# Another order of the query blocks in the attention stage of a two-layer trunk

## The chip, the cores and the metric

The kernel runs on one core of one Trainium2 chip. The metric is the device time of one execution in microseconds (us), as the median of several runs. The engines are TensorE (PE, with its weight loads as PEld), VectorE (DVE), ScalarE (ACT), GpSimd (POOL) and SyncE (SP), which issues the DMAs. Each takes its instructions in the order of the program.

## The reference

Two layers over x of shape (1, 1024, 1024) in fp32. Layer 0 is a gMLP and a pooling mixer, layer 1 a latent attention with 16 heads; each ends with an output projection, a residual and a layer norm. The change lies in the attention of layer 1, cut to this:

```python
    def attend_block(args):
        ql, qr, i = args
        s = jnp.einsum('bqhr,bkr->bhqk', ql, kv_c) + jnp.einsum('bqhd,bkd->bhqk', qr, k_rope)
        s = s.astype(jnp.float32) * ATTN_SCALE
        q_chunk = (i * Q_BLOCK + jnp.arange(Q_BLOCK)) // CHUNK
        mask = key_chunk[None, :] <= q_chunk[:, None]
        p = jax.nn.softmax(jnp.where(mask, s, -jnp.inf), axis=-1).astype(kv_c.dtype)
        return jnp.einsum('bhqk,bkr->bqhr', p, kv_c)

    o_lat = lax.map(attend_block, (q_lat_b, q_rope_b, jnp.arange(nb)))
    ...
    o = jnp.einsum('bshr,rhd->bshd', o_lat, w_uv).reshape(B, S, MLA_WIDTH)
    return (o * jax.nn.silu(z)) @ w_out
```

There are 8 blocks of 128 queries. Block i sees the keys of blocks 0 to i alone, so block 7 has eight times the scores of block 0. The blocks don't depend on each other, so they can be done in any order.

## The kernel before, in words

Precision: each fp32 operand of a product is kept as two parts, a rounded high part and the rest. `split` makes them from a PSUM tile (L120: a cast on ACT; L121: a subtraction on DVE), and `mm3` makes a product from three matmuls (L112 to L114).

The attention stage runs from about 910 us to 1377 us. The 16 heads are done in four groups of four; an item is one group g and one block i of queries, and there are 32 items in the order of the list `items` (L1745). An item has three generators, each of which is run in pieces:

- `gen_q`: for an odd block the latent queries of that block and the one below it (qlp, 24 matmuls, split into qlh and qll), then for every block the rotary part (qrp; rope on DVE and POOL; qrs; four transposes qrt; qrT).
- `gen_s`: for each of the four heads five score matmuls (L1785 to L1789; twice that for more than 512 keys) into a double PSUM bank sc. DVE masks the diagonal (L1821) and takes the maximum nm (L1824), ACT makes the exponential p with its row sum (L1832), DVE the reciprocal rz, POOL the normalised p (L1836). The blocks 1 and 0 do two heads in one tile sc, with lines of their own (L1798, L1800, L1804, L1809). There are two such double banks in all, so a tile sc takes the bank of the tile two before it, and that is free when the exponential has read it.
- `gen_v`: for each block j of keys four transposes of p (pt, L1853), split into pth, and three matmuls into av; the transposes run one block of keys ahead. Then av is split into oh and ol, and for an even block both blocks of the pair go through 12 matmuls uvp, are multiplied by the gate zt (L1877) and stored to o_d.

Tiles are named by group, block and head or key block: sc363 is group 3, block 6, head 3; pt110 is group 1, block 1, key block 0; oh31 is group 3, pair 1 (blocks 3 and 2).

A list of times places the pieces: item m's queries at about m, its scores at m + 2, its values at m + 3.3. So the scores of one item run beside the values of the item before it in the list. Group weights come once in a group, and the first loads and splits of the output projection (r1W, r1A; f1B00 and f1A00 are two of its operands) at fixed times near the end. From this the program's scheduler sets the order on every engine. After the attention comes the output projection, which reads o_d, then the residual and the layer norm.

Of the kernel before, what the change touches and what calls it, by code (L numbers as in the profile page):

```python
# [24 lines left out]
NG = H // GH  # L25
# [55 lines left out]
def trunk_kernel(ctx, tc, x, c, positions, ada_w, ada_b, ln_g, ln_b, e_w_in, gmlp_norm_g,  # L81
# [1621 lines left out]
    def gen_q(g, i, first, last):  # L1703
# [32 lines left out]
        for h in range(GH):  # L1736
# [4 lines left out]
        qrT[g, i] = qt  # L1741
        yield

    down = [7, 6, 5, 4, 3, 2, 1, 0]
    items = [(g, i, i % 2 == 1, i % 2 == 0) for g in range(NG)  # L1745
             for i in (down if g + 1 < NG else down[2:] + down[:2])]
    q_first = gen_q(*items[0])
    turns += [lambda: drain(q_first, 1) for _ in range(3)]

# [170 lines left out]
    for m in range(n):  # L1920
        g, i, first, last = items[m]
# [67 lines left out]
```

## Time and profile before

| | us |
|---|---|
| median of 3 runs (lowest to highest) | 1525.44 (1524.47 to 1526.9) |
| the profiled execution | 1528.2 |
| span of its trace | 1526.4 |
| PE busy in the span | 1478.0 (97%) |
| DVE, POOL, ACT busy | 1047.3, 652.0, 622.8 |
| mean granted clock of PE | 0.99 |

Busy time counts the instructions' own durations. Matmuls overlap, so two starts can be closer than the duration of one; what a matmul costs is the distance to the next start. The granted clock is a share of the full 2.4 GHz.

### The profile page before, as it was taken

The page shows a single profiled execution, that of the slowest core. Times are in us where ns is not written, and L with a number is a line of the kernel's source. Part 1 is how long each engine was busy: PE and PEld are TensorE (multiplying, and loading weights), DVE is VectorE, ACT ScalarE, POOL GpSimd, SP SyncE. Part 2 cuts the span into 40 slices and gives each one's busy share as a digit, 9 for nine tenths or more (in the row PEclk, how much of TensorE's full clock was granted, in tenths as well). Part 3 has the DMA queues.
Part 4 walks back from the last instruction along what each step waited for, and adds up shares of the span by engine and source line. Part 5 has one row for each costly group of instructions (what it writes and reads, how often), then busy time and mean ns, then how long its engine had stood idle before and what let it go on. Part 6 is the DMA issues. An engine that isn't in the chain of part 4 may idle for free.

```text
span 1526.4 us, 21181 instructions
## 1 busy us (share of the span) xinstructions
PE 1478.0 (97%) x7875; PEld 1269.7 (83%) x7875; DVE 1047.3 (69%) x1660; ACT 622.8 (41%) x1122; POOL 652.0 (43%) x583
## 2 busy tenths in 40 slices
PE   7999998999999999999999999999999999999997
PEld 5888776998898888888888878898989889878885
DVE  6557859574567596556766446777777777668598
ACT  3433323323323323425433445554544545555351
POOL 0033427376567023115776632454444442234245
PEclk9999999999999999999999999999999999999999
DMA  9725543103202799612375551131231131274532
GB/s 300 193 70 200 200 173 110 57 28 111 83 28 90 277 383 333 232 56 77 111 275 193 193 162 59 56 111 42 70 97 56 56 103 33 94 261 139 179 125 97
DMA packets 130771, 210.47 MB, mean 138 GB/s; under 512 B 11774, under 2 KB 78052, under 8 KB 130668
## 3 DMA queue, kind: packets, MB, share of 16 engines
q1 hardware_dynamic: 130668, 209.12, 40.5%
q8 instruction: 62, 1.02, 0.3%
q14 instruction: 41, 0.34, 0.1%
HBM read 152.46 MB, written 56.63 MB: 137 GB/s over the span
## 4 chain that ended last, share of the span: by engine, by line
PE 79%; DVE 9%; DMA 5%; issue 2%; ACT 2%; SPq 1%; POOL 1%; DVEq 0%; POOLq 0%; ACTq 0%
PE pt L1853 4%; PE y L113 3%; PE y L114 3%; PE y L112 3%; PE sc L1785 2%; PE av L113 2%; PE av L112 2%; PE av L114 2%; PE sc L1787 2%; PE sc L1786 2%; PE sc L1789 2%; PE sc L1788 2%; PE zb L113 2%; PE zb L114 2%; DVE mc L753 1%
## 5 line engine op out<-in xcount | busy, mean ns | idle before, releaser
L1836 POOL TENSOR_SCALAR p<-p,rz 128x1024 f32<-128x1024 f32 (+5 forms) x96 | 82.3, 858 | 175.3 <-DVE rz L1835 157.4
L120 ACT CAST pth<-pt 128x512 fp32r<-128x512 f32 x144 | 82.0, 590 | 79.9 <-PE pt L1853 78.9
L121 DVE TENSOR_TENSOR pth<-pt,pth 128x512 fp32r<-128x512 f32 x144 | 96.1, 687 | 24.6 <-ACT pth L120 23.7
L1832 ACT ACTIVATE p<-sc,nm 128x1024 f32<-128x1024 f32 (+5 forms) x96 | 81.8, 853 | 57.4 <-DVE nm L1824 45.9
L1824 DVE TENSOR_REDUCE nm<-sc 128x1 f32<-128x1024 f32 (+5 forms) x96 | 85.1, 887 | 2.0 <-DVE rz L1835 0.2
L1853 PE MATMUL pt<-ident,p 128*128 128x128 f32 x576 | 84.6, 272 | 0.1
L1853 PEld LDWEIGHTS pt<-ident,p 128*128 128x128 f32 x576 | 69.6, 140 | 11.3 <-DVE ol L121 0.3
L1785 PE MATMUL sc<-kvTh,qlh 128*128 128x512 f32 (+4 forms) x192 | 70.6, 368 | 8.3 <-ACT p L1804 3.2
L1431 POOL TENSOR_TENSOR ws<-ws,ws 128x1024 f32<-128x1024 f32 x16 | 43.4, 2724 | 75.0 <-DVE ws L1426 51.8
L1788 PE MATMUL sc<-KRh,qrT 128*128 128x512 f32 (+4 forms) x192 | 66.7, 348 | 0.0
L1789 PE MATMUL sc<-KRl,qrT 128*128 128x512 f32 (+4 forms) x192 | 66.4, 346 | 0.0
L1787 PE MATMUL sc<-kvTh,qll 128*128 128x512 f32 (+4 forms) x192 | 66.3, 345 | 0.0
L1786 PE MATMUL sc<-kvTl,qlh 128*128 128x512 f32 (+4 forms) x192 | 66.1, 344 | 0.0
L112 PE MATMUL av<-pth,kvh 128*128 128x512 f32 x144 | 61.1, 425 | 1.0 <-ACT pth L120 1.0
L113 PE MATMUL av<-pth,kvh 128*128 128x512 f32 x144 | 60.2, 418 | 0.2 <-DVE pth L121 0.2
L114 PE MATMUL av<-pth,kvl 128*128 128x512 f32 x144 | 56.7, 394 | 0.0
L753 DVE SCALAR_TENSOR_TENSOR mc<-mw,cT,mc 128x1024 f32<-128x1024 f32 x28 | 47.5, 1698 | 9.2 <-DMA mw<-in_ada_w_dram 8.8
L1245 POOL TENSOR_TENSOR r1A<-r1A,r1A 128x1024 f32<-128x1024 f32 x12 | 32.3, 2700 | 44.7 <-DMA r1A<-o_d 34.8
L121 DVE TENSOR_TENSOR ol<-av,oh 128x512 fp32r<-128x512 f32 x32 | 22.0, 687 | 39.7 <-ACT oh L120 39.7
L1785 PEld LDWEIGHTS sc<-kvTh,qlh 128*128 128x128 f32 x192 | 36.5, 190 | 14.6 <-ACT p L1832 5.6
L120 ACT CAST oh<-av 128x512 fp32r<-128x512 f32 x32 | 18.8, 587 | 60.1 <-PE av L114 59.7
L1550 POOL TENSOR_TENSOR qrf<-qrf 128x256 f32<-128x256 f32 x32 | 23.6, 737 | 44.6 <-DVE rz L1835 20.1
(1887 smaller groups left out, 5147.8 us busy)
## 6 DMA issues: line engine op xcount, KB each, us to landing
mw<-in_ada_w_dram SPq DMA_DIRECT2D x32, 512.0 KB
r0W<-in_e_w_out_dram SPq DMA_DIRECT2D x32, 512.0 KB
wf_d<-ws SPq DMA_DIRECT2D x28, 512.0 KB
r1W<-wf_d SPq DMA_DIRECT2D x28, 512.0 KB
ada<-in_ada_w_dram SPq DMA_DIRECT2D x32, 256.0 KB
r0A<-mix_d SPq DMA_DIRECT2D x16, 512.0 KB
ws<-in_o_w_out_dram SPq DMA_DIRECT2D x16, 512.0 KB
z_d<-zo SPq DMA_DIRECT2D x16, 512.0 KB
```

The costliest lines, as they stand in the source:

```text
L112: PE.matmul(ps, lhsT=lh, rhs=rh, start=start, stop=False, skip_group_check=more)
L113: PE.matmul(ps, lhsT=lh, rhs=rl, start=False, stop=False, skip_group_check=more)
L114: PE.matmul(ps, lhsT=ll, rhs=rh, start=False, stop=stop, skip_group_check=more)
L120: A.copy(out=hi, in_=src)
L121: eng.tensor_tensor(out=lo, in0=src, in1=f(hi), op=ALU.subtract)
L1785: PE.matmul(o, lhsT=qh[:, h, qs], rhs=kvTh[:, ks], start=True, stop=False)
L1786: PE.matmul(o, lhsT=qh[:, h, qs], rhs=kvTl[:, ks], start=False, stop=False)
L1787: PE.matmul(o, lhsT=qo[:, h, qs], rhs=kvTh[:, ks], start=False, stop=False)
L1788: PE.matmul(o, lhsT=qt[:, h, :], rhs=KRh[:, ks], start=False, stop=False)
L1789: PE.matmul(o, lhsT=qt[:, h, :], rhs=KRl[:, ks], start=False, stop=True)
L1824: V.tensor_reduce(out=nm, in_=sv, axis=AX.XY, op=ALU.max, negate=True)
L1853: PE.transpose(ps[:, h, :], pl[h][:, j * P:(j + 1) * P], ident)
```

## The change

The order of the blocks in `items` is another. Before it is 7, 6, 5, 4, 3, 2, 1, 0 for the first three groups of heads and 5, 4, 3, 2, 1, 0, 7, 6 for the last. After it is 7, 6, 1, 0, 5, 4, 3, 2 and 5, 4, 1, 0, 3, 2, 7, 6. Pairs stay together, and first and last block of the stage stay what they were. Lines behind it move up by one (L1785 is L1784 after).

```diff
@@ -1741,9 +1741,8 @@
         qrT[g, i] = qt
         yield
 
-    down = [7, 6, 5, 4, 3, 2, 1, 0]
     items = [(g, i, i % 2 == 1, i % 2 == 0) for g in range(NG)
-             for i in (down if g + 1 < NG else down[2:] + down[:2])]
+             for i in ((7, 6, 1, 0, 5, 4, 3, 2) if g + 1 < NG else (5, 4, 1, 0, 3, 2, 7, 6))]
     q_first = gen_q(*items[0])
     turns += [lambda: drain(q_first, 1) for _ in range(3)]
```

Where before the scores of block 7 met the values of block 0, those of block 5 (in the last group of block 3) do now, and the scores of the next group's block 7 meet the values of block 2. In the last group block 7 comes behind block 2 instead of block 0. Three places show how the instructions move.

First listing: DVE in the last group, at the scores of block 6. nm is the maximum of a score tile, f1B00l and f1A00l are subtractions for the output projection. Before:

```order
L1824 TENSOR_REDUCE nm360_12666<-sc360_12654 128x1
L1877 TENSOR_TENSOR zt30_11986<-uvp300_12617,zt30_11986 128x512
L1877 TENSOR_TENSOR zt30_11986<-uvp301_12625,zt30_11986 128x512
L1835 RECIPROCAL rz360_12671<-zs360_12669 128x1
L121 TENSOR_TENSOR f1B00l_12675<-r1W00_12442,f1B00h_12674 128x1024
L1821 MEMSET sc361_12682 64x64
L121 TENSOR_TENSOR f1A00l_12679<-r1A110_12444,f1A00h_12678 128x1024
L1824 TENSOR_REDUCE nm361_12694<-sc361_12682 128x1
L1821 MEMSET sc362_12757 64x64
```

After:

```order
L1823 TENSOR_REDUCE nm360_12666<-sc360_12654 128x1
L1820 MEMSET sc361_12682 64x64
L1823 TENSOR_REDUCE nm361_12694<-sc361_12682 128x1
L1834 RECIPROCAL rz360_12671<-zs360_12669 128x1
L1876 TENSOR_TENSOR zt31_11977<-uvp310_12617,zt31_11977 128x512
L121 TENSOR_TENSOR f1B00l_12675<-r1W00_12384,f1B00h_12674 128x1024
L1876 TENSOR_TENSOR zt31_11977<-uvp311_12625,zt31_11977 128x512
L121 TENSOR_TENSOR f1A00l_12679<-r1A110_12386,f1A00h_12678 128x1024
L1834 RECIPROCAL rz361_12699<-zs361_12697 128x1
```

The two subtractions stood ahead of the maximum of sc361; now this maximum comes first.

Second listing: PE in the first group, at the values of block 1. Before:

```order
L1853 MATMUL pt010_8824<-ident_88,p010_8673 128x128 x2
L1853 MATMUL pt010_8824<-ident_88,p011_8774 128x128 x2
L1853 MATMUL pt011_8832<-ident_88,p010_8673 128x128 x2
L1853 MATMUL pt011_8832<-ident_88,p011_8774 128x128 x2
L1788 MATMUL sc170_8877<-KRh_7380,qrT17_8764 128x512
L1789 MATMUL sc170_8877<-KRl_7381,qrT17_8764 128x512
L1785 MATMUL sc170_8877<-kvTh_7396,qlh13_8632 128x512
L1786 MATMUL sc170_8877<-kvTl_7397,qlh13_8632 128x512
L1787 MATMUL sc170_8877<-kvTh_7396,qll13_8633 128x512
L1788 MATMUL sc170_8877<-KRh_7380,qrT17_8764 128x512
L1789 MATMUL sc170_8877<-KRl_7381,qrT17_8764 128x512
```

After:

```order
L1852 MATMUL pt010_8111<-ident_88,p010_7913 128x128 x2
L1852 MATMUL pt010_8111<-ident_88,p011_8044 128x128 x2
L1852 MATMUL pt011_8119<-ident_88,p010_7913 128x128 x2
L1852 MATMUL pt011_8119<-ident_88,p011_8044 128x128 x2
L112 MATMUL av01_8110<-pth010_8116,kvh_7412 128x512
L113 MATMUL av01_8110<-pth010_8116,kvh_7412 128x512
L114 MATMUL av01_8110<-pth010_8116,kvl_7413 128x512
L112 MATMUL av01_8110<-pth011_8124,kvh_7412 128x512
L113 MATMUL av01_8110<-pth011_8124,kvh_7412 128x512
L114 MATMUL av01_8110<-pth011_8124,kvl_7413 128x512
L1737 MATMUL qrt04_8131<-identR_107,qrs04_8088 128x128 x4
L112 MATMUL qlp010_8200<-q0h_7289,wa00_7344 128x256
```

The seven score matmuls between the transposes and the first matmul av are no longer there; behind av come the transposes qrt and then the 24 matmuls qlp.

Third listing: the last group at the scores of block 7, first ACT (casts and exponentials), then PE. ACT before:

```order
L120 CAST oh30_12483<-av31_12485 128x4x128
L1804 ACTIVATE p301_12535,zs301_12536<-sc301_12515,nm301_12533 128x128 x2
L1832 ACTIVATE p370_12557,zs370_12558<-sc370_12543,nm370_12555 128x1024
L1832 ACTIVATE p371_12577,zs371_12578<-sc371_12563,nm371_12575 128x1024
L120 CAST pth300_12589<-pt300_12584 128x512
```

ACT after:

```order
L120 CAST pth333_12492<-pt333_12487 128x512
L120 CAST oh31_12432<-av33_12434 128x4x128
L1831 ACTIVATE p370_12535,zs370_12536<-sc370_12521,nm370_12533 128x1024
L1831 ACTIVATE p371_12555,zs371_12556<-sc371_12541,nm371_12553 128x1024
L120 CAST pth320_12567<-pt320_12562 128x512
```

PE before:

```order
L1785 MATMUL sc371_12563<-kvTh_7396,qlh33_12297 128x512
L1786 MATMUL sc371_12563<-kvTl_7397,qlh33_12297 128x512
L1787 MATMUL sc371_12563<-kvTh_7396,qll33_12298 128x512
L1788 MATMUL sc371_12563<-KRh_7380,qrT37_12424 128x512
L1789 MATMUL sc371_12563<-KRl_7381,qrT37_12424 128x512
L1853 MATMUL pt300_12584<-ident_88,p301_12535 128x128
L1785 MATMUL sc372_12597<-kvTh_7396,qlh33_12297 128x512
```

PE after:

```order
L112 MATMUL av33_12434<-pth333_12492,kvh_7412 128x512
L1788 MATMUL sc371_12541<-KRl_7381,qrT37_12368 128x512
L1852 MATMUL pt320_12562<-ident_88,p322_12481 128x128 x2
L113 MATMUL av33_12434<-pth333_12492,kvh_7412 128x512
L114 MATMUL av33_12434<-pth333_12492,kvl_7413 128x512
L1852 MATMUL pt321_12570<-ident_88,p322_12481 128x128 x2
L1784 MATMUL sc372_12592<-kvTh_7396,qlh33_12256 128x512
```

Before, the cast oh30 and the exponentials of block 0 stood ahead of p370, with all of sc371 to come on PE behind av; now the cast oh31 waits for the end of av33, and the first matmul of sc372 follows that with two transposes between.

## Rows read from the trace of the kernel before

**Rows 1.** The page's busy time by engine; and its chain's shares by engine.

```profile
PE 1478.0 (97%) x7875; PEld 1269.7 (83%) x7875; DVE 1047.3 (69%) x1660; ACT 622.8 (41%) x1122; POOL 652.0 (43%) x583
...
PE 79%; DVE 9%; DMA 5%; issue 2%; ACT 2%; SPq 1%; POOL 1%; DVEq 0%; POOLq 0%; ACTq 0%
```

**Rows 2.** Stretches: length, busy us (instructions) of each engine, granted clock, DMA share, GB/s.

```profile
920.00:1035.00 115.00, 114.50 (x731) 102.92 (x730) 83.16 (x187) 60.21 (x134) 47.98 (x57) 1.00 0.21 69
...
1338.00:1345.00 7.00, 4.91 (x18) 4.03 (x17) 4.43 (x9) 2.06 (x4) 1.01 (x1) 0.76 0.39 138
1345.00:1420.00 75.00, 75.00 (x363) 62.23 (x361) 58.59 (x52) 41.54 (x55) 34.49 (x14) 1.00 0.62 214
```

**Rows 3.** What PE waits for, 900 to 1420 us: us in total, times, longest.

```profile
PE sc L1785 <- ACT p L1804: 3.2, 4, 1.4
PE sc L1785 <- ACT p L1832: 3.0, 4, 2.1
...
PE sc L1785 <- DVE qrf L1549: 2.1, 1, 2.1
...
PE av L112 <- ACT pth L120: 1.0, 4, 0.2
```

**Rows 4.** Timeline around the longest wait: start, duration, instruction, [idle time before]. DVE, ACT, PE.

```profile
1335.95 1.48 DVE L121 TENSOR_TENSOR f1B00l<-r1W,f1B00h 128x1024 fp32r<-128x1024 f32 x1 [0.70 <-ACT f1B00h L120]
1337.46 1.20 DVE L121 TENSOR_TENSOR f1A00l<-r1A,f1A00h 128x1024 fp32r<-128x1024 f32 x1
1338.59 1.07 DVE L1824 TENSOR_REDUCE nm<-sc 128x1 f32<-128x896 f32 x1
...
1339.77 1.01 ACT L1832 ACTIVATE p<-sc,nm 128x896 f32<-128x896 f32 x1 [2.91 <-DVE sc L1821]
...
1338.46 0.37 PE L1789 MATMUL sc<-KRl,qrT 128*128 128x448 f32 x1
1340.92 0.48 PE L1785 MATMUL sc<-kvTh,qlh 128*128 128x448 f32 x1 [2.09 <-ACT p L1832]
...
1344.56 0.45 PE L112 MATMUL av<-pth,kvh 128*128 128x512 f32 x1
```

**Rows 5.** Timeline at 1134 us, ACT and then PE.

```profile
1134.99 0.59 ACT L120 CAST oh<-av 128x512 fp32r<-128x512 f32 x1 [2.36 <-PE av L114]
1135.47 0.37 ACT L1804 ACTIVATE p<-sc,nm 128x128 f32<-128x128 f32 x1
...
1134.51 0.39 PE L114 MATMUL av<-pth,kvl 128*128 128x512 f32 x1
1136.34 0.50 PE L1785 MATMUL sc<-kvTh,qlh 128*128 128x512 f32 x1 [1.44 <-ACT p L1804]
1136.68 0.39 PE L1786 MATMUL sc<-kvTl,qlh 128*128 128x512 f32 x1
```

**Rows 6.** Timeline of PE at 1032 us, from block 0 to block 7.

```profile
1031.98 0.40 PE L1789 MATMUL sc<-KRl,qrT 128*128 128x512 f32 x1
1032.65 0.50 PE L1785 MATMUL sc<-kvTh,qlh 128*128 128x512 f32 x1 [0.27 <-ACT p L1832]
```

**Rows 7.** Timeline of PE at 1245 us: transposes with other matmuls behind them.

```profile
1245.36 1.04 PE L1853 MATMUL pt<-ident,p 128*128 128x128 f32 x8
1246.15 0.42 PE L1788 MATMUL sc<-KRh,qrT 128*128 128x384 f32 x1
```

**Rows 8.** Timeline of PE at two places where av follows its transposes directly.

```profile
999.64 1.03 PE L1853 MATMUL pt<-ident,p 128*128 128x128 f32 x8
1000.91 0.50 PE L112 MATMUL av<-pth,kvh 128*128 128x512 f32 x1 [0.24 <-ACT pth L120]
...
1223.39 1.04 PE L1853 MATMUL pt<-ident,p 128*128 128x128 f32 x8
1224.67 0.50 PE L112 MATMUL av<-pth,kvh 128*128 128x512 f32 x1 [0.24 <-ACT pth L120]
1225.39 0.50 PE L113 MATMUL av<-pth,kvh 128*128 128x512 f32 x1 [0.22 <-DVE pth L121]
```

## The prediction

> **What bounds the kernel now.** I read the page's engine table and chain first: TensorE (PE) is busy 97% of the span and makes 79% of the chain that ended last [rows 1]. In such a kernel a reordering pays only by what it does to PE's idle time, so the next view is the busy time of stretches [rows 2]. In the attention items PE is busy nearly all of the time (114.50 of the 115 us from 920 to 1035); the poorest stretch is 1338 to 1345, with 4.91 of 7 us busy and a granted clock of 0.76. From 1345 to 1420 PE is busy for 75.00 of 75 us, so what is won or lost before 1345 is carried on; behind it come only the output projection and the layer norm, which the change doesn't touch.
>
> The third view lists what PE waits for between 900 and 1420 [rows 3]. Nearly all of it is one kind: the first score matmul (sc, L1785) waits until the exponentials (p, L1804 for the blocks 1 and 0, L1832 for the others) have emptied its PSUM bank. There are two double banks for scores, so a score tile waits for the exponential of the tile two before it. Four waits on L1804 sum to 3.2 us, four on L1832 to 3.0 us, the longest 2.1 us; the one on DVE is the start of the stage and stays. A wait costs more than its idle time, so I price it from start to start: the time between two PE starts, less what the same step takes where nothing waits (0.23 us for a matmul over 512 columns, 0.20 over 448).
>
> **What the change removes.** The PE instructions are the same ones in both kernels. (1) The largest wait is at 1338.46: the score tile sc363 starts at 1340.92, 2.46 us after the matmul before it, where the step is 0.20 us otherwise: 2.26 us [rows 4]. Why: VectorE (DVE) runs in program order and does the two subtractions f1B00l (1.48 us) and f1A00l (1.20 us) of the next stage's operands ahead of the maximum of sc361; so that starts at 1338.59 only, the exponential at 1339.77, and the bank is free at 1340.92. After the change the maximum of sc361 stands ahead of both subtractions (first order listing), and between the last matmul of sc361 and the first of sc363 PE has, besides the ten matmuls of sc362, twelve matmuls uvp (0.12 each) and eight transposes of block 7 (0.79 by [rows 7]): 2.0 + 1.44 + 0.79, about 4.2 us, against the 2.33 us from the start of the maximum to the free bank. So this wait goes and I see nothing late in its place. (2) The clock: behind that wait the ten matmuls from 1340.92 to 1344.56 take 3.64 us in place of 10 x 0.205 [rows 4]: 1.59 us, at the lower clock. It goes with the wait. (3) Of the four waits on L1804 two come where block 1's values and block 7's scores meet, two a little earlier, at block 0's scores. At 1134.51 the last matmul of av11 starts; ScalarE (ACT) casts its result (0.59), then runs the two exponentials of sc101, and only then is the bank of sc271 free: 1.83 us from start to start less 0.23, so 1.60 [rows 5], which is 0.16 more than its idle time of 1.44. The other three too have casts ahead of the exponentials (oh, and at block 0's scores two casts qlh of the next pair); I price the four by the sum of their idle time [rows 3] and 0.16 each, 3.2 + 0.64. In the new order the casts qlh come later, and the exponentials of block 0 still stand behind a cast oh, but PE then has the transposes qrt and 24 matmuls qlp between (second listing): at 0.12 us each that is 2.9 us, more than the cast and the exponentials together. Between the groups 0 and 1 the kernel before has qlp there already, and sc171 isn't among the four waits. Sum 3.84. (4) Without the longest, the L1832 waits have 0.9 us of idle time left in three places. Two of them are at the fourth head of block 7 behind block 0, one of these at 1031.98: 0.67 from start to start less 0.23, so 0.44 [rows 6]. That step no longer exists: 2 x 0.45. **Gone: 2.26 + 1.59 + 3.84 + 0.90 = 8.6 us.**
>
> **What the change adds.** (5) A new wait of the same kind as (3), in the last group, where blocks 2 and 7 meet (third listing). ACT has the cast oh31 (of block 3's values) ahead of the exponential of sc370, and PE needs the bank of sc370 for sc372 directly after the end of av33. Let T be the start of the last matmul of av33. By [rows 5] the cast starts 0.48 after it and the next exponential 0.48 after that; by [rows 4] an exponential over 896 elements frees its bank 1.15 us after its start, and I add 0.11 for 1024: T + 2.22. PE has that matmul and two transposes, 0.23 + 0.17 (half of what four take), and then waits: 1.8 us. Behind it on PE stand all of sc372, sc373 and block 2's values; none of it can be pulled ahead. (6) Block 1's values. There PE does eight transposes (pt), ACT casts the results to fp32r, DVE subtracts the rest, and six matmuls av use them. In the kernel before, other matmuls stand between: at 1245.36 eight transposes are followed at 0.79 us by score matmuls, with no wait [rows 7]. In the new order av follows directly (second listing). The trace shows such a place twice: at 999.64 the gap is 1.27, so 0.48 is lost, and at 1223.39 it is 1.28, and the next matmul comes 0.72 after the first, in place of the 0.34 behind another wait [rows 5], so 0.87 [rows 8]. Bounds 0.48 and 0.87 each; below nothing is excluded, since the same matmuls then follow later. I take 0.75, nearer to the second, whose DVE has the same multiplications of zt ahead of the subtraction. Four groups: 3.0 us (1.9 to 3.5). (7) Small waits. I went along PE's new order and summed, at the durations above, PE's work between a producer's input and the use of its result; at twelve places it is 0.3 to 1 us shorter than the producers' work: eight score tiles (sc053, sc153, sc253, sc130, sc230, sc370, sc322, sc333) and four transposed tiles (of blocks 5, 4 and 6). The nearest row for the first is that of (4), for the second the 0.48 of (6): 8 x 0.44 + 4 x 0.48 = 5.4 us. Ends: 0, because a wait gives the producers time to catch up and so takes the next one's place, and 8 x 0.44 + 4 x 0.87 = 7.0. (8) DMA: the loads of the last stage are issued a little earlier and the stores of o_d come in another order; the longest rows of PE's waits name ACT and DVE, none a DMA [rows 3], so nothing. **Added: 1.8 + 3.0 + 5.4 = 10.2 us.**
>
> The sum is + 1.6 us. The profiled execution took 1528.2 us (span 1526.4 us), 2.8 above the median of 1525.44, so the median of the changed kernel comes to **1527.0 us**: not to be told from no change, since a measurement of this kernel can tell about 0.2%, 3.05 us.
>
> **A rule against the change.** The rows show PE's clock falling behind the idle time of 2.09 us (0.76 in that stretch) [rows 2, 4], and not behind the one of 1.44 us, where the matmul after the first takes 0.39 again [rows 5]. The Trainium skill, "TensorE: Matmul & The Clock Gate", Part 1, says that the throttled state is the default and that only activity releases it; by that alone idle time costs the clock as well, and the sum would be + 1.6 + 1.59 = + 3.2; by the row at 1.44 us it stays + 1.6. The new 1.8 us lies between the two rows, so the trace leaves it open; it is the second rival.
>
> **Rivals.** First, **faster**: the small waits of (7) don't come, because each is short against what ACT and DVE catch up behind the waits that stay, and (6) costs 0.48 each. Then 1.8 + 1.9 - 8.6 = - 4.9, so 1520.5 us. For it: DVE is busy 69% and ACT 41% [rows 1], so on average they aren't behind; against it: PE waited for them at the eight places of (3) and (4) all the same. Chance 0.25. Second, **slower**: at sc372, behind the new wait of 1.8 us, the clock falls as it does at 1340.92, which costs another 1.59, with (6) at 0.87 each. It decides if the clock behind this wait does as behind the one of 2.09 us [rows 4], and not if as behind that of 1.44 us [rows 5]. 1.8 + 1.59 + 3.5 + 5.4 - 8.6 = + 3.7, so 1529.1 us. Chance 0.27. Third, **the wait of sc363 moves instead of going**: the subtractions f1B00l and f1A00l now lie ahead of the memset and maximum of sc362, and if the transposes of block 6 then come before its normalised tiles, up to the 3.85 us of (1) and (2) return: + 1.6 + 3.85, so 1530.9 us. Against it: block 7's eight rounds of transposes and matmuls lie between. Chance 0.06.
>
> **How the numbers follow.** The forecast keeps 0.42. Range: from a little below rival one's 1520.5 to rival three's 1530.9, so 1520.0 to 1531.0; it leaves out the part of rival one in which still more goes, and little above. Faster by over 0.2% (under 1522.4) is rival one, 0.25; slower by over 0.2% (over 1528.5) are two and three, 0.33; within it 0.42.
>
> **What would show it.** The trace after should have no idle PE at sc363 and no stretch of low clock there; no wait over 0.5 us on L1804 (L1803 then); a wait near 1.8 us of sc on the exponential of L1831 in the last group, with or without a low clock behind it; and in each group a wait of av on pth behind eight transposes. If the waits of PE in the attention stage sum to less than the 7.2 us of sc on ACT and of av before by several us, rival one holds. I am wrong if the time moves by more than 4 us while these waits stay as said, for then something outside PE's waits decides, such as the last stretch or the loads.

## The result, and the profile after

| us | before | after |
|---|---|---|
| median (lowest to highest) of 4 runs each | 1524.95 (1522.89 to 1526.90) | 1535.06 (1533.23 to 1537.41) |
| the profiled execution | 1528.2 | 1535.73 |
| span of its trace | 1526.4 | 1534.0 |
| PE busy | 1478.0 | 1482.1 |

The ratio is 1.0073, with a 95% interval of 1.0059 to 1.0087: slower by 9 to 13 us. The forecast was 1527.0 and the range ended at 1531.0, so the prediction was wrong; "slower" had a chance of 0.33, and its time in the rivals was 4 to 6 us too low.

The two profiled executions differ by 7.5 us. All of it lies in the attention items: from the first score matmul of block 6 in the first group to the first matmul y1c of the output projection the trace of before shows 478.19 us and that of after 485.93, 7.74 more; what follows y1c takes 120.4 us in both. The medians lie 10.1 us apart, so one trace of each kernel shows most of the loss and not all of it. I use this stretch below as **the stretch**, since the whole time of one kernel scatters by several us from run to run.

The stretches of after that answer to [rows 2]; the columns are length, then busy us (instructions) of PE, PEld, DVE, ACT and POOL, granted clock, DMA share, GB/s:

```profile
920.00:1035.00 115.00, 113.83 (x726) 101.86 (x724) 82.11 (x186) 58.52 (x131) 47.85 (x57) 1.00 0.20 69
...
1338.00:1345.00 7.00, 6.96 (x35) 5.85 (x34) 4.16 (x8) 3.79 (x7) 2.22 (x2) 1.00 0.01 2
```

The hole at 1338 with its low clock is gone: 6.96 of 7 us are busy there, at a clock of 1.00. But the stretch from 920 to 1035 has lost 0.67 us of busy time against [rows 2]. The list of what PE waits for, 918 to 1440 us, after (us in total, times, longest), says why:

```profile
PE sc L1784 <- ACT p L1831: 4.8, 8, 1.6
PE av L113 <- DVE pth L121: 2.6, 11, 0.3
PE av L112 <- ACT pth L120: 2.6, 9, 0.6
```

Against [rows 3] the four waits on the exponentials of L1804 (now L1803) are gone, those on L1831 have become eight, and av waits 20 times for its operands pth, on ACT or on DVE, 5.2 us in all. Before, it waited 1.0 us on ACT in four places [rows 3] and once on DVE, by the same list of before:

```profile
PE av L113 <- DVE pth L121: 0.2, 1, 0.2
```

Priced from start to start, as in the prediction, PE's steps in the stretch lost this (places with at least 0.13 us):

| PE instruction that came late | before, us | after, us |
|---|---|---|
| av | 2.6 | 12.3 |
| sc (with the slow clock of before) | 9.4 | 7.3 |
| others | 1.0 | 1.0 |
| sum | 13.0 | 20.6 |

The difference of the sums, 7.6 us, is that of the stretch (7.7). The prices hang a little on the step that is taken as the one without a wait: with the usual step of each pair of matmuls that follow each other, av comes to 11.6 after the change, the sums to 13.0 and 20.0. So PE's waits account for nearly all of the loss in these two traces: the scores gained 2.1 us and the values lost 9.0 to 9.7.

### The profile page after: what moved, and what is told of

It is laid out like the page before. It is cut to its first block, busy times and chain, and to the rows that moved or that the text cites. A ratio compares the mean times of both kernels' runs of the same rounds, so it can differ in the third digit from the quotient of the medians.

```text
span 1534.0 us, 21199 instructions
## 1 busy us (share of the span) xinstructions
PE 1482.1 (97%) x7875; PEld 1267.3 (83%) x7875; DVE 1042.1 (68%) x1660; ACT 622.5 (41%) x1122; POOL 651.5 (42%) x583
## 4 chain that ended last, share of the span: by engine, by line
PE 74%; DVE 12%; DMA 5%; issue 3%; ACT 3%; POOL 2%; SPq 1%; DVEq 0%; POOLq 0%; ACTq 0%
PE pt L1852 3%; PE y L113 3%; PE y L114 3%; PE y L112 3%; PE av L113 2%; PE sc L1784 2%; PE sc L1785 2%; PE sc L1786 2%; PE sc L1787 2%; PE av L114 2%; PE sc L1788 2%; PE av L112 2%; PE zb L113 2%; PE zb L114 1%; PE y1a L114 1%
## 5 line engine op out<-in xcount | busy, mean ns | idle before, releaser
L121 DVE TENSOR_TENSOR pth<-pt,pth 128x512 fp32r<-128x512 f32 x144 | 95.9, 686 | 29.6 <-ACT pth L120 28.4
L1831 ACT ACTIVATE p<-sc,nm 128x1024 f32<-128x1024 f32 (+5 forms) x96 | 81.7, 853 | 44.4 <-DVE nm L1823 32.4
L1784 PE MATMUL sc<-kvTh,qlh 128*128 128x512 f32 (+4 forms) x192 | 70.2, 366 | 7.0 <-ACT p L1831 4.8
L1785 PE MATMUL sc<-kvTl,qlh 128*128 128x512 f32 (+4 forms) x192 | 65.9, 343 | 0.0
L112 PE MATMUL av<-pth,kvh 128*128 128x512 f32 x144 | 62.0, 430 | 2.6 <-ACT pth L120 2.6
L113 PE MATMUL av<-pth,kvh 128*128 128x512 f32 x144 | 61.6, 428 | 2.9 <-DVE pth L121 2.6
L1784 PEld LDWEIGHTS sc<-kvTh,qlh 128*128 128x128 f32 x192 | 36.3, 189 | 13.2 <-ACT p L1831 8.7
```

Of the source, the lines that this page charges most:

```text
L112: PE.matmul(ps, lhsT=lh, rhs=rh, start=start, stop=False, skip_group_check=more)
L113: PE.matmul(ps, lhsT=lh, rhs=rl, start=False, stop=False, skip_group_check=more)
L121: eng.tensor_tensor(out=lo, in0=src, in1=f(hi), op=ALU.subtract)
L1784: PE.matmul(o, lhsT=qh[:, h, qs], rhs=kvTh[:, ks], start=True, stop=False)
L1785: PE.matmul(o, lhsT=qh[:, h, qs], rhs=kvTl[:, ks], start=False, stop=False)
```

## The experiments

The theories. A: the loss comes from the first three groups. B: from the last one. W: from the weights of the next group, whose splits now lie beside larger blocks. C: from neighbours of unlike size. D: from the small blocks' own values. E: a transposed tile costs time when PE has too little other work between its transposes (pt) and the first matmul that uses it (av), for then the cast on ACT and the subtraction on DVE aren't done in time. F: DVE and ACT are short of time as such, so what is hidden here is waited for there. Each measured change of the stretch is against the 478.19 us of before; ratios are against the kernel before on the same chip.

For E I counted in each kernel's order of PE instructions the work between the last of a tile's four transposes and the first av with it, at the distances of the rows (0.23 us for 512 columns, 0.12 for 256, 0.09 for a transpose). Of 144 tiles this was under 0.9 us for 5 in the kernel before and for 22 in the changed one. The prediction had priced 11 of these 22: both tiles of block 1 in four groups, pt150, pt344 and pt360. Four, the first tiles of block 3, were there before. Seven it had not named: the last tiles of block 6 in three groups, pt131, pt153, pt331 and pt332.

**Which groups.** The new order in the last group alone:

```diff
-             for i in (down if g + 1 < NG else down[2:] + down[:2])]
+             for i in (down if g + 1 < NG else [5, 4, 1, 0, 3, 2, 7, 6])]
```

And in the first three alone:

```diff
-             for i in (down if g + 1 < NG else down[2:] + down[:2])]
+             for i in ([7, 6, 1, 0, 5, 4, 3, 2] if g + 1 < NG else down[2:] + down[:2])]
```

> The new order in the last group of heads alone; the first three go 7 to 0 as before. Theory A (the loss lies in the first three groups, where the matmuls av now wait for their operands pth; the last group gains): from the traces the last group, from the first scores of its block 5 to the first matmul y1c of the output projection, went from 163.65 us to 161.44 us, so 2 us below the kernel before, about 1522.8 us, with no wait at sc363 and a wait of about 1.6 us at sc372. Rival B (the loss comes from the changed last group, by its new waits): 1527 us or more.

> The new order in the first three groups alone; the last goes 5, 4, 3, 2, 1, 0, 7, 6 as before. Theory A: from the first scores to the first scores of the last group the traces show 332.3 us before and 342.3 us after, so 10 us above the kernel before, about 1535 us; the wait at sc363 with its low clock is there again. Rival B: within 2 us of the kernel before, about 1525 us.

Last group alone: ratio 1.0009 (1.0000 to 1.0018), stretch + 0.95 us. First three alone: 1.0040 (1.0026 to 1.0053), + 5.4 us. The two add up to 6.4 of the 7.7 us. The loss lies mostly in the first three groups, as A says, though A had expected 10 us there; but the last group doesn't gain, as A had it from two traces whose pieces didn't end at the same work: its waits on sc fall from 9.4 to 6.7 us and its waits of av rise from 2.6 to 5.8. The waits of PE, 918 to 1440 us, in the trace with the last group alone (two of the waits on L1804 are those of the unchanged groups):

```profile
PE sc L1785 <- ACT p L1832: 2.6, 4, 1.6
PE sc L1785 <- ACT p L1804: 2.0, 2, 1.4
PE av L112 <- ACT pth L120: 1.5, 5, 0.6
PE av L113 <- DVE pth L121: 1.1, 5, 0.2
```

**The weights.** The next group's weights two items earlier in the changed kernel:

```diff
-QO, QW, VO, VW, PT, PS, PW = 0, 1.2, 0.3, 0.6, -0.5, 0.6, 4
+QO, QW, VO, VW, PT, PS, PW = 0, 1.2, 0.3, 0.6, -0.5, 0.6, 2
```

> The changed kernel, with the next group's weights (splits on ACT and POOL) prepared two items earlier: beside blocks 1, 0 and 5 instead of beside 5, 4 and 3. Rival W (the weights' work, which lay beside small blocks before and lies beside blocks 5 and 4 now, keeps POOL and ACT from the scores and the values): the waits at sc153 and sc253 (1.0 us each from start to start) and those of av13, av15 and av25 go, 1528 to 1531 us. Theory A (it is the order of the blocks itself): within 1.5 us of the changed kernel, 1533.5 to 1536.5 us.

Ratio 1.0058 (1.0045 to 1.0072), stretch + 9.8 us, av still 11.7 us late in all. W is out.

**The price of the largest wait of before.** The kernel before, with the first splits of the output projection later:

```diff
-WO, WS, RO, RS, RP = -0.25, 0.75, 4.5, 3, 0.2
+WO, WS, RO, RS, RP = 0.0, 0.75, 4.5, 3, 0.2
```

> The kernel before, with the first loads and splits of the output projection a quarter of an item later (WO 0.0 instead of -0.25), so that the two subtractions f1B00l and f1A00l stand behind the maxima of sc361 and sc362. If the price of that wait is right (2.26 us, and 1.59 us at the lower clock behind it, with nothing late in its place): 1521.1 us. If the work that is put off is missed later on (the output projection waits for it): within 1 us of the kernel before, 1524 to 1526 us.

Ratio 1.0006 (0.9995 to 1.0016), stretch - 0.9 us. The wait at sc363 shrank from 2.09 to 0.35 us of idle time and the clock stayed up; but the same two subtractions then stood ahead of the first pth of block 7. DVE, then PE, in this run (start, duration, instruction, idle time before):

```profile
1340.15 1.20 DVE L121 TENSOR_TENSOR f1B00l<-r1W,f1B00h 128x1024 fp32r<-128x1024 f32 x1
1341.27 1.22 DVE L121 TENSOR_TENSOR f1A00l<-r1A,f1A00h 128x1024 fp32r<-128x1024 f32 x1
1342.49 0.11 DVE L1821 MEMSET sc<- 64x64 f32 x1
1342.52 1.26 DVE L121 TENSOR_TENSOR pth<-pt,pth 128x512 fp32r<-128x512 f32 x2
...
1339.19 0.47 PE L1785 MATMUL sc<-kvTh,qlh 128*128 128x448 f32 x1 [0.35 <-ACT p L1832]
...
1341.56 0.50 PE L112 MATMUL av<-pth,kvh 128*128 128x512 f32 x1
1341.89 0.60 PE L1853 MATMUL pt<-ident,p 128*128 128x128 f32 x4
1343.24 0.50 PE L113 MATMUL av<-pth,kvh 128*128 128x512 f32 x1 [0.75 <-DVE pth L121]
```

The subtractions f1B00l and f1A00l run from 1340.15 to 1342.49; the pth behind them starts at 1342.52, and av waits 0.75 us for it. From start to start the scores lost 2.9 us less than before, av 1.1 us more, and the output projection's first matmuls, which now wait for a later split, 0.8 us more: two thirds of the gain came back as other waits. Nearly half of the 2.9 us is the low clock of the trace of before, which the same wait doesn't always bring (see (2) below).

**More work between.** The transposes two blocks of keys ahead instead of one, in the changed kernel and in the kernel before:

```diff
-        pts = [tr(0)]
+        pts = [tr(j) for j in range(min(2, i + 1))]
         for j in range(i + 1):
-            if j < i:
-                pts.append(tr(j + 1))
+            if j + 2 <= i:
+                pts.append(tr(j + 2))
```

> The changed kernel with the transposes of the values two blocks of keys ahead instead of one. In the changed kernel the waits of av on pth cost some 13 us from start to start, against 2.6 us before the change. Theory E (they are waits of time alone: between pt and its av there is too little other work for the cast and the subtraction to end): most of them go, 8 us or more below the changed kernel, so at most 3 us above the kernel before. Rival F (DVE and ACT have more work in these stretches than PE, and what is hidden here is waited for elsewhere, at the scores): within 2 us of the changed kernel, 8 us or more above the kernel before.

> The kernel before with the same: transposes two blocks of keys ahead. Theory E: only the waits of av03, av13, av23 and av33 can go, 2.4 us in all, so 0 to 2.4 us below the kernel before. Rival F: the third tile in PSUM keeps a bank from the queries, 1 us or more above it.

Changed kernel: ratio 1.0021 (1.0008 to 1.0035), stretch + 2.1 us, so 5.7 us of the 7.7 came back. The tiles with under 0.9 us of cover fell from 22 to 7, the lateness of av from 12.3 to 4.4 us. That is E and not F, though E had expected 8 us or more back and the queries now wait on DVE (qrs):

```profile
PE sc L1784 <- ACT p L1831: 2.7, 5, 0.8
PE qrt L1737 <- DVE qrs L121: 1.2, 2, 1.0
PE sc L1784 <- ACT p L1803: 1.0, 4, 0.4
PE av L113 <- DVE pth L121: 0.9, 4, 0.3
```

Kernel before: ratio 1.0044 (1.0027 to 1.0061), stretch + 5.4 us. av loses only 1.1 us instead of 2.6, but the transposes qrt, the matmuls uvp and, a little, the scores lose some 5 us that they hadn't lost. Here E's forecast failed and F's came true: in this kernel the hiding of av's waits costs more elsewhere than it gives. Its waits:

```profile
PE sc L1785 <- ACT p L1832: 3.3, 6, 1.7
PE qrt L1737 <- DVE qrs L121: 3.0, 3, 1.8
PE sc L1785 <- ACT p L1804: 2.8, 4, 1.4
PE uvp L113 <- DVE ol L121: 0.7, 3, 0.2
```

The queries' transposes wait 3.0 us on the split of the query (DVE qrs), where the kernel before has one such wait of 0.4 us. That the third tile takes a PSUM bank from the queries is my reading, and no run shows the bank by itself.

**Other orders.** Two further orders in the first three groups, with the last as before:

```diff
-             for i in (down if g + 1 < NG else down[2:] + down[:2])]
+             for i in ([7, 6, 5, 4, 1, 0, 3, 2] if g + 1 < NG else down[2:] + down[:2])]
```

```diff
-             for i in (down if g + 1 < NG else down[2:] + down[:2])]
+             for i in ([7, 6, 3, 2, 5, 4, 1, 0] if g + 1 < NG else down[2:] + down[:2])]
```

> First three groups in the order 7, 6, 5, 4, 1, 0, 3, 2, last group as before. Blocks 1 and 0 stand before 3 and 2 and no longer before the next group's 7, as in the change, but beside block 4's values instead of block 6's, and block 3's scores beside block 0's values instead of block 5's. Theory C (the loss comes from neighbours of unlike size: scores of a small block beside the values of a large one and the other way): a third of the loss of the run with the first three groups changed, 1 to 2.5 us above the kernel before. Theory D (it comes from the small blocks' own values, which are next to nothing that covers them unless block 7's scores follow): 5 to 7 us above it, as in that run.

> First three groups in the order 7, 6, 3, 2, 5, 4, 1, 0, last group as before. Blocks 1 and 0 keep their place before the next group's 7, but block 3's scores lie beside block 6's values and block 5's scores beside block 2's values. Theory C (unlike neighbours): 3 to 6 us above the kernel before. Theory D (the small blocks): within 1.5 us of it.

Ratios 1.0062 (1.0047 to 1.0077) and 1.0055 (1.0036 to 1.0074), stretch + 8.1 and + 6.1 us. The first, above what either theory had forecast, speaks against C as the one cause, since its neighbours are less unlike than those of the change and the loss is larger; the second, at the end of C's range, speaks against D, since its small blocks keep their place. What both have in common with the changed kernel is the number of badly covered tiles, 15 and 11, and av that loses 8.5 and 6.7 us. Unlike neighbours and small blocks in a new place are each a way to leave tiles uncovered.

**E by its own numbers.** Two ahead only in blocks 3, 5 and 6 of the changed kernel:

```diff
-        pts = [tr(0)]
+        ahead = 2 if i in (3, 5, 6) else 1
+        pts = [tr(j) for j in range(min(ahead, i + 1))]
         for j in range(i + 1):
-            if j < i:
-                pts.append(tr(j + 1))
+            if j + ahead <= i:
+                pts.append(tr(j + ahead))
```

The same with `i == 3` in the kernel before; this together with the late splits; and at last the kernel before with the values placed earlier against the scores:

```diff
-QO, QW, VO, VW, PT, PS, PW = 0, 1.2, 0.3, 0.6, -0.5, 0.6, 4
+QO, QW, VO, VW, PT, PS, PW = 0, 1.2, 0.2, 0.6, -0.5, 0.6, 4
```

> The changed kernel with the transposes two blocks of keys ahead only in the values of blocks 3, 5 and 6. Theory E, in numbers: a transposed tile with less than 0.9 us of other PE work between its transposes and its av costs about 0.55 us (by the order, the kernel before has 5 such tiles, the changed one 22, the run with the last group alone 11, the one with the first three 16; av waited 2.6, 12.3, 5.8 and 8.9 us). Here there are 12, so some 6.5 us of av waits, and without the waits of the queries for a PSUM bank that the run with two ahead everywhere had: 1 to 4 us above the kernel before. Rival F: as the changed kernel, 9 us or more above.

> The kernel before with the transposes two ahead only in the values of block 3, whose first tile is the one with least cover in each group. Theory E: the waits of av03, av13, av23 and av33, 2.4 us in all, fall by half or more; 1 to 2 us below the kernel before. Rival (the third tile's PSUM bank is missed by the queries as in the run with two ahead everywhere): 0 to 2 us above.

> The run before this with the first splits of the output projection a quarter of an item later (as in the run with the late splits, which took 0.9 us from the stretch up to the output projection). Theory E: 2 to 3 us below the kernel before. Rival: nothing, within 1 us.

> The kernel before, in its old order of blocks, with the values placed a tenth of an item earlier against the scores (VO 0.2 instead of 0.3). By the order 27 transposed tiles then have less than 0.9 us of other PE work between their transposes and their av, against 5. Theory E: some 27 x 0.55 us of av waits instead of 2.6, so 8 to 13 us above the kernel before, though no block has another neighbour. Theory C (it is the neighbours' sizes and not the cover): within 2 us.

The first: ratio 1.0046 (1.0028 to 1.0063), stretch + 5.0 us. av lost 8.5 us with 12 such tiles, where 6.5 were expected, and the stretch came out above the 1 to 4 us of E; the direction was right, the size not. Block 3 alone: 1.0013 (1.0002 to 1.0025), + 2.0 us. Here E's forecast failed: av lost 2.3 us instead of 2.6, and qrt 0.8 and sc 2.1 us more than before. With the late splits: 1.0005 (0.9994 to 1.0017), + 0.9 us, where E had 2 to 3 us below the kernel before; it failed here too. No kernel of mine was faster than the one before.

The values earlier: ratio 1.0201 (1.0180 to 1.0222), stretch + 28.4 us, more than twice the upper end of what I had expected, with not one block moved. The waits:

```profile
PE sc L1785 <- ACT p L1832: 10.9, 11, 1.3
PE av L112 <- ACT pth L120: 9.8, 20, 0.7
PE qrt L1737 <- DVE qrs L121: 3.7, 3, 2.8
...
PE av L113 <- DVE pth L121: 0.9, 4, 0.2
```

av waits 20 times on ACT and four times on DVE, and loses 17.6 us from start to start, where 27 x 0.55, so 14.9, had been expected. What I hadn't foreseen is the rest: the scores and qrt, now later against the values, lose 9 us more than in the kernel before. So the cover of the transposed tiles is a cause in itself; that it is not the only one, this run shows as well. Over the kernels (the one with both small edits, with 4 such tiles, is left out) the badly covered tiles and the lateness of av go together:

| kernel | tiles under 0.9 us | av late, us | stretch, us |
|---|---|---|---|
| before | 5 | 2.6 | 478.2 |
| late splits, before | 5 | 3.7 | - 0.9 |
| two ahead, before | 0 | 1.1 | + 5.4 |
| block 3 two ahead, before | 4 | 2.3 | + 2.0 |
| two ahead, changed | 7 | 4.4 | + 2.1 |
| last group alone | 11 | 5.8 | + 0.9 |
| unlike sizes | 11 | 6.7 | + 6.1 |
| small blocks later | 15 | 8.5 | + 8.1 |
| two ahead in 3, 5, 6, changed | 12 | 8.5 | + 5.0 |
| first three groups alone | 16 | 8.9 | + 5.4 |
| weights earlier, changed | 21 | 11.7 | + 9.8 |
| changed | 22 | 12.3 | + 7.7 |
| values earlier | 27 | 17.6 | + 28.4 |

Where there are ten or more such tiles, av loses 0.5 to 0.7 us for each on average. The stretch follows only as far as the scores and the queries don't move too.

Tile by tile the count is a rougher guide than that. Of the 22 tiles of the changed kernel, twelve lost 8.8 us and ten lost nothing over 0.13 us at a matmul: pt011, pt111, pt211 and the seven that the prediction had not named. The other 2.8 us were lost at eight tiles with 1.05 to 1.8 us of cover, all of them at L113, which waits for DVE. So the average mixes tiles that lost 0.4 to 1.0 us with tiles that lost none, and the count leaves out the way to L113 by DVE. One of the ten is pt066:

```profile
958.62 0.60 PE L1852 MATMUL pt<-ident,p 128*128 128x128 f32 x4
...
960.07 0.39 PE L112 MATMUL av<-pth,kvh 128*128 128x512 f32 x1
```

Its av starts at 960.07 without a wait, because L113 of the tile before it (pt065, cover 1.05) had come 0.29 us late, at 959.50, and in that time the cast of pt066 was done.

## Why the prediction was wrong, point by point

(1), (2) Right for this kernel: nothing waits at sc363, and the clock stays up. PE and DVE after the change, where the last matmul of sc361 starts at 1344.71 and sc363 begins at 1349.26 without a wait:

```profile
1344.71 0.36 PE L1788 MATMUL sc<-KRl,qrT 128*128 128x448 f32 x1
...
1349.05 0.37 PE L1788 MATMUL sc<-KRl,qrT 128*128 128x448 f32 x1
1349.26 0.36 PE L1784 MATMUL sc<-kvTh,qlh 128*128 128x448 f32 x1
...
1345.15 0.11 DVE L1820 MEMSET sc<- 64x64 f32 x1 [0.79 <-PE sc L1788]
1345.30 1.09 DVE L1823 TENSOR_REDUCE nm<-sc 128x1 f32<-128x896 f32 x1
...
1346.97 1.67 DVE L121 TENSOR_TENSOR f1B00l<-r1W,f1B00h 128x1024 fp32r<-128x1024 f32 x1
```

The maximum of sc361 starts at 1345.30, directly behind its matmuls, and the subtraction f1B00l after it at 1346.97, where before it came first [rows 4]. The run with the late splits shows that avoiding the wait is not by itself a gain: it stays one only if nothing needs DVE where the subtractions then stand.

The 1.59 us of (2) were in part luck of the one trace that the prediction read. The same wait is there in the runs with the first three groups alone, with the small blocks later and with the unlike sizes, with 2.09 to 2.15 us of idle time, and the clock stayed at 1.00 behind it each time, though I had expected it low again in the first of them; with block 3 two ahead it fell again (0.53 from 1344.70 to 1348.30, at 2.15 us). PE in the run with the first three groups alone:

```profile
1347.44 0.47 PE L1785 MATMUL sc<-kvTh,qlh 128*128 128x448 f32 x1 [2.09 <-ACT p L1832]
...
1349.37 0.36 PE L1789 MATMUL sc<-KRl,qrT 128*128 128x448 f32 x1
```

The av behind these ten matmuls starts at 1349.56, so they take 2.12 us and not 3.64 [rows 4]. Against a trace of before with the clock up, the stretches of the changed kernel and of all the others but block 3 two ahead would come out some 1.5 us worse. How often the kernel before runs with the low clock there, its one trace doesn't show.

(3) Right: no wait on L1803 is left; 3.84 forecast, 4.1 measured. (4) Half wrong: the two waits of block 7's fourth head are gone where they were, but at sc273, where block 7 now follows block 2, 0.20 us became 0.55.

(5) Right to a few hundredths: 1.8 us forecast, 1.78 measured. ACT, then PE:

```profile
1331.53 0.58 ACT L120 CAST oh<-av 128x512 fp32r<-128x512 f32 x1 [5.55 <-PE av L114]
1332.01 1.12 ACT L1831 ACTIVATE p<-sc,nm 128x1024 f32<-128x1024 f32 x1
...
1331.10 0.39 PE L114 MATMUL av<-pth,kvl 128*128 128x512 f32 x1
1331.33 0.38 PE L1852 MATMUL pt<-ident,p 128*128 128x128 f32 x2
1333.28 0.50 PE L1784 MATMUL sc<-kvTh,qlh 128*128 128x512 f32 x1 [1.56 <-ACT p L1831]
1333.61 0.39 PE L1785 MATMUL sc<-kvTl,qlh 128*128 128x512 f32 x1
```

av33's last matmul starts at 1331.10, the cast oh31 0.43 us later, the exponential of sc370 0.48 after that, and sc372 at 1333.28.

The second rival, that the clock falls there, didn't happen: the matmul after the first takes 0.39 us. The Trainium skill, "TensorE: Matmul & The Clock Gate", Part 1, has the throttled state as the default, which activity releases. The low clock behind the 2.09 us [rows 4] agrees with that. But the idle stretches of 1.44 us [rows 5] and 1.56 us here left the clock alone, that of 2.09 us did so in other runs (see (2)), and the longest one of the attention, 2.77 us in the run with the values earlier, left it at 1.00 as well. So in these traces idle time can bring the throttled state back and need not, and its length alone doesn't decide it.

(6) Mis-sized. In each of the four groups two losses came, together over the upper bound of 0.87. PE at the values of block 1 in the second group:

```profile
1079.02 1.03 PE L1852 MATMUL pt<-ident,p 128*128 128x128 f32 x8
1080.29 0.49 PE L112 MATMUL av<-pth,kvh 128*128 128x512 f32 x1 [0.24 <-ACT pth L120]
1081.02 0.50 PE L113 MATMUL av<-pth,kvh 128*128 128x512 f32 x1 [0.23 <-DVE pth L121]
```

From the transposes to av 1.27 us instead of 0.79, then 0.73 to the next matmul instead of 0.23: 0.98. In the first three groups it is so (0.98 to 1.03); in the last, L113 came late at both tiles, 0.89 in all. The four groups lost 3.9 us where 3.0 were forecast and 3.5 was the upper bound. That bound was too low since I took the step behind another wait (0.34) as the one without a wait.

(7) **The step that failed.** For the scores it was near: eight places, 4.5 us against 3.5. For the transposed tiles it named four places and 1.9 us; av lost 9.7 us more than before, of which (6) is 3.9, so 5.8 us. Tile by tile (with the finer steps, so 9.0 and 5.1): pt150, pt344 and pt360, which it had priced, lost 1.9 us; eight tiles with 1.05 to 1.8 us of cover lost 2.8; and at block 3 L113 now comes late in two groups where before it was one, 0.5. What it missed is thus one matmul of the three, L113, and the engine it waits for, DVE. The way over both engines, at pt344, the values of block 4 in the last group (ACT, DVE, PE):

```profile
1293.69 0.59 ACT L120 CAST pth<-pt 128x512 fp32r<-128x512 f32 x1 [1.72 <-PE pt L1852]
...
1294.31 0.69 DVE L121 TENSOR_TENSOR pth<-pt,pth 128x512 fp32r<-128x512 f32 x1 [0.89 <-ACT pth L120]
...
1293.06 0.60 PE L1852 MATMUL pt<-ident,p 128*128 128x128 f32 x4
...
1294.33 0.50 PE L112 MATMUL av<-pth,kvh 128*128 128x512 f32 x1
1295.06 0.50 PE L113 MATMUL av<-pth,kvh 128*128 128x512 f32 x1 [0.22 <-DVE pth L121]
```

Four transposes start at 1293.06 and three matmuls of the tile before follow. The cast runs from 1293.69 to 1294.28, and only then the subtraction, from 1294.31. L112 needs the cast alone and starts at 1294.33, 0.15 us late; L113 needs the subtraction and starts at 1295.06, 0.50 us late. The prediction left out places that came out under 0.3 us short, and priced a late tile by its first matmul (0.48); the longer way over two engines to L113 it had at block 1 alone. By this way three of the eight tiles came late, pt065, pt165 and pt265, 0.9 us together. In the list above L113 stands with 11 waits on DVE, against one before.

A second kind I had not priced at all: DVE is busy with something else, the maximum of a score tile. It is behind the other five of the eight, pt171, pt271, pt251, pt351 and pt322, 1.9 us together. At block 7's values in the second group the cover is ample (1.8 us), but the maximum stands first (ACT, DVE, PE):

```profile
1048.88 0.59 ACT L120 CAST pth<-pt 128x512 fp32r<-128x512 f32 x1 [0.86 <-PE pt L1852]
...
1049.49 1.09 DVE L1823 TENSOR_REDUCE nm<-sc 128x1 f32<-128x896 f32 x1
1050.50 0.68 DVE L121 TENSOR_TENSOR pth<-pt,pth 128x512 fp32r<-128x512 f32 x1
...
1048.25 0.60 PE L1852 MATMUL pt<-ident,p 128*128 128x128 f32 x4
...
1050.54 0.46 PE L112 MATMUL av<-pth,kvh 128*128 128x512 f32 x1
1051.23 0.50 PE L113 MATMUL av<-pth,kvh 128*128 128x512 f32 x1 [0.24 <-DVE pth L121]
```

The cast is done by 1049.5, the maximum takes DVE until 1050.5, and L113 comes at 1051.23, 0.46 us late.

The first rival held that one wait would spare the next. It did so at some tiles, such as block 1's second tile in three groups, but not in the sum: the small waits of (7) came, and more of them than were forecast. The third rival didn't come about. DMA (8) is in no row of PE's waits, as said.

## What to carry to other kernels

A large wait that a reordering takes away is easy to see in the trace; what it adds is spread over many places of half a us, and here these outweighed it. Before such a change, count in the new order, for every tile that goes PE, ACT, DVE and back to PE, the PE work between its making and its use, for each of the producers in the chain and not for the first alone, and look for what stands ahead of them on DVE. An order that looks arbitrary may be the one in which each engine's work happens to cover the others', and here no other order that was tried made the kernel faster.

## What the runs showed of the hardware

A wait of av that the profile lists with 0.24 us of idle time costs 0.46 to 0.49 us from start to start, since matmuls that follow each other overlap in the rows (0.39 us long, 0.23 apart) and the one behind a wait doesn't: the 20 listed waits of av are 5.2 us in the list and 9.9 us in the time.

Idle time of PE of about 2.1 us at the same place, sc363, lowered the granted clock in two traces (before, and block 3 two ahead) and left it at 1.00 in three. Where it fell, ten matmuls took 1.5 us longer.

The median of the kernel before was 1524.95, 1526.36, 1526.47 and 1527.58 us in the four sets of runs, so a comparison of a few us needs runs of both kernels on the same chip, and the sum over a stretch of the trace tells what the times alone do not.
